# Hybrid layer on one core: modulation loads on GpSimd's queue, shared buffers left to the weights, padded tables cleared at the start

## The chip, the cores and the metric

One core of a Trainium2 chip runs the kernel. The metric is the device time of one execution in microseconds (us), and the median of several runs is compared.

The core has a TensorE (PE: matmuls), a VectorE (DVE), a ScalarE (ACT) and a GpSimd (POOL), and a SyncE (SP) that in this kernel issues DMA transfers only. Each engine works through its own instructions in a fixed order and waits at an instruction until what it needs is there. A transfer is issued by an instruction of one engine, and is then carried out by 16 DMA engines.

## The reference

```python
mod = (jax.nn.silu(c) @ w_ada + b_ada)[:, None, :]      # c: 2048, w_ada: 2048 x 12288
sh1, sc1, g1, sh2, sc2, g2 = jnp.split(mod, N_MOD, axis=-1)

h = rms_norm(x, norm1_g) * (1.0 + sc1) + sh1            # x: 256 x 2048
proj = h @ w_in                                          # 2048 x 4096
q, k, v, u = jnp.split(proj, [ATTN_WIDTH, 2 * ATTN_WIDTH, 3 * ATTN_WIDTH], axis=-1)
...
attn = dilated_attention(q, k, v)                        # 8 heads, three dilations
y = jax.nn.gelu(s5_mixer(u, ...))                        # 64 groups of 16 channels, 64 complex states
ssm = y * jax.nn.sigmoid(y @ w_glu + b_glu)

mixed = jnp.concatenate([rms_norm(attn, attn_out_g), rms_norm(ssm, ssm_out_g)], axis=-1) @ w_out
x = x + g1 * mixed
h2 = rms_norm(x, norm2_g) * (1.0 + sc2) + sh2
ff = jnp.square(jax.nn.relu(h2 @ w_ff1)) @ w_ff2         # 2048 -> 8192 -> 2048
return x + g2 * ff
```

One sequence of 256 positions, all in float32. Nearly 300 MB of weights are read, 100 MB of them `w_ada`.

## The kernel before

**Weights.** A weight product is made of three matmuls over a high and a low part of both factors (`mm3`, L194 to L196). A weight comes in halves of 512 KB (128x1024) through `k.raw` (L179, issued by SP) into the tag `raw`, which has 5 buffers; ACT rounds it into `wh` (L162), DVE takes the rest into `wl` (L137), each with 3 buffers, and both must be done before PE reads them.

**The modulation.** `w_ada` is read in 96 pieces of 1 MB (128x2048). `pump(n)` calls for n pieces, at a rate by stage (`PUMPS`). Pieces of 12 of the 24 blocks go to PE as four matmuls each (L260, into `tr`), the other half to DVE as multiplications with a sum (L159). After four pieces a block of 512 modulation values is done (L271 turns a row into columns, L137 adds the bias into `mod`).

**Places of the pieces.** `ada_raw` gives a piece its place. The first 16 take the places that `FIRST` names: tiles of later stages which stand empty at the start (`Q`, `K`, `U`, `V`, `TO` and `CA` in two halves, `WB0`, `WB1`, `PD`). A later one takes the next name of its stage's list in `RINGS`; where that is `raw`, the piece comes as two halves through `k.raw` and shares the 5 buffers with the weights, and in the stages of the MLP that is the only name. Loads of whole pieces are issued at L242 (`FIRST`) and L248 (`RINGS`), by SP.

```python
FIRST = ("Q", "K", "U", "V", "TO", "TO", "CA", "CA", "WB0", "WB1", "PD", "Q", "K", "TO", "TO", "CA")
RINGS = (("cbc", "K"), ("cbc", "PD", "raw", "raw"), ("cbc", "raw", "raw"), ("HA", "U", "WB0"), ("HA", "PD"))
```

**The start.** Eight pieces give scale and shift of the first 512 columns; beside them ACT squares x (L308) and PE sums (L311, L314). From these come `HA` (L332, L333), and with it the first `w_in` matmul. DVE makes the tables of the S5 mixer out of `bb` and `cc` (tiles `V`, `CA`, `WB2`, `WB3`, `T0`); ACT copies them into padded tables (`padB` in `PD`, `padCs` in `WB0` and `WB1`, cleared by GpSimd at L604), PE multiplies these (L532) and ACT takes the result to the Toeplitz table `TO`, whose empty part GpSimd clears at L612. Two smaller clearings by GpSimd are at L498 (`wpad` in `PD`) and L550 (state `H`).

**What sets the order.** The kernel is written with a tile framework: tiles of one tag share buffers, and a tile's first writer waits for the last reader of the tile before it. A scheduler places the instructions of every engine in a fixed order by a simulated time, so an edit can move instructions of engines that it doesn't name. SP keeps that order for all its loads: a load that waits for its place holds up those behind it. Each queue also has eight counters for loads under way, and its ninth load waits for the first to land.

Of the kernel before, what the change touches and what calls it, by code (L numbers as in the profile page):

```python
# [16 lines left out]
P = 128  # L17
# [9 lines left out]
RAW = 5  # L27
FIRST = ("Q", "K", "U", "V", "TO", "TO", "CA", "CA", "WB0", "WB1", "PD", "Q", "K", "TO", "TO", "CA")
RINGS = (("cbc", "K"), ("cbc", "PD", "raw", "raw"), ("cbc", "raw", "raw"), ("HA", "U", "WB0"), ("HA", "PD"))
PUMPS = (4.0, 2.0, 1.0, 1.0, 0.75, 0.5, 1.0, 0.5, 0.5, 2.5, 1.0, 2.0, 1.0, 0.4)  # L30
# [11 lines left out]
SUB = [0, 2, 1, 3]  # L42
# [75 lines left out]
class _K:  # L118
# [5 lines left out]
    def t(self, tag, shape, dt=F32, bufs=1):  # L124
        self.n += 1
        return self.sb.tile(list(shape), dt, name=f"{tag}_{self.n}", tag=tag, bufs=bufs)
# [72 lines left out]
def _body(nc, tc, I, out, sb, ps):  # L199
    k = _K(nc, tc, I, out, (sb, ps))  # L200
    t, tr = k.t, k.tr
# [16 lines left out]
    sigc = t("sigc", [P, 16])  # L218
    nc.scalar.activation(sigc, col["c"], AF.Sigmoid)
    cpad = t("cpad", [P, 16, 32])  # L220
    nc.vector.memset(cpad, 0.0)
# [8 lines left out]
    def ada_raw(src):  # L230
        if ring["first"] < len(FIRST):
            tag = FIRST[ring["first"]]
            if tag in ("TO", "CA"):
                if tag in halves:
                    raw = halves.pop(tag)[:, 4:8]
# [5 lines left out]
            ring["first"] += 1  # L241
            nc.sync.dma_start(raw, src.rearrange("p (a n) -> p a n", a=4))  # L242
            return [raw]
        ring["i"] += 1
        tag = ring["tags"][ring["i"] % len(ring["tags"])]
        if tag not in ("raw", "T0"):
            raw = t(tag, [P, 4, NB])
            nc.sync.dma_start(raw, src.rearrange("p (a n) -> p a n", a=4))  # L248
            return [raw]
# [134 lines left out]
    s5 = {}  # L384
# [110 lines left out]
    def wb_block(i):  # L495
        if i == 0:
            s5["wpad"] = t("PD", [P, 8, 2, 4, 2, 16])
            nc.gpsimd.memset(s5["wpad"], 0.0)  # L498
        wpad, w, rr = s5["wpad"], i // 2, slice(8 * (i % 2), 8 * (i % 2) + 8)
# [48 lines left out]
    def state_in():  # L548
        H = t("XT", [P, 2, 32, 64])
        nc.gpsimd.memset(H[:, :, :, 0:1].rearrange("p i r c -> p i (r c)"), 0.0)  # L550
        for r2 in range(0, 32, 4):
# [48 lines left out]
    ring["tags"] = RINGS[0]  # L600
    padB = t("PD", [P, 32, 2, 2, 16])
    padCs = [t(f"WB{i}", [P, 8, 2, 2, 4, 16]) for i in range(2)]
    for w in (padB, *padCs):
        nc.gpsimd.memset(w, 0.0)  # L604
    for w in range(2):
# [4 lines left out]
    for b in range(1, 4):  # L610
        tz = toep[32 * b : 32 * b + 32].rearrange("p r g s j -> p (r g) (s j)")
        nc.gpsimd.memset(tz[:, :, 0 : 16 * SUB[b]], 0.0)  # L612
    ca = t("CA", [P, 32, 2, 4, 16])
# [42 lines left out]
    H = state_in()  # L656
# [396 lines left out]
```

## Time and profile before

| | us |
|---|---|
| three runs | 1320.88, 1320.88, 1313.66 |
| median of them | 1320.88 |
| profiled execution, its own time | 1312.4 |
| span of its trace | 1310.6 |
| PE busy in the span | 1210.9 |
| DVE busy | 867.9 |
| ACT busy | 579.7 |
| GpSimd busy | 13.1 |

Busy time counts an engine's own instructions; register, semaphore and DMA-issuing ones are left out. The profiled execution is one more run, 1.3 us below the fastest of the three and 8.5 below their median.

### The profile page before, as it was taken

The page shows a single profiled execution, that of the slowest core. Times are in us where ns is not written, and L with a number is a line of the kernel's source. Part 1 is how long each engine was busy: PE and PEld are TensorE (multiplying, and loading weights), DVE is VectorE, ACT ScalarE, POOL GpSimd, SP SyncE. Part 2 cuts the span into 40 slices and gives each one's busy share as a digit, 9 for nine tenths or more (in the row PEclk, how much of TensorE's full clock was granted, in tenths as well). Part 3 has the DMA queues.
Part 4 walks back from the last instruction along what each step waited for, and adds up shares of the span by engine and source line. Part 5 has one row for each costly group of instructions (what it writes and reads, how often), then busy time and mean ns, then how long its engine had stood idle before and what let it go on. Part 6 is the DMA issues. An engine that isn't in the chain of part 4 may idle for free.

```text
span 1310.6 us, 19312 instructions
## 1 busy us (share of the span) xinstructions
PE 1210.9 (92%) x7618; PEld 1020.9 (78%) x7618; DVE 867.9 (66%) x1383; ACT 579.7 (44%) x783; POOL 13.1 (1%) x12
## 2 busy tenths in 40 slices
PE   5867999999986799798989999999999999999898
PEld 1445766776675799798888888888888888888787
DVE  4666245599778675666768755975576666668754
ACT  3467734333357444344335444443344443343432
POOL 0110000000000000000000000000000000000000
PEclk9988999999879799899999999999999999999999
DMA  9936487747777245657887566765677656677763
GB/s 380 417 141 253 167 329 259 277 162 264 291 286 263 107 153 179 204 193 254 278 289 239 177 192 212 267 202 188 193 239 229 222 185 188 222 218 261 257 208 100
DMA packets 76122, 299.67 MB, mean 229 GB/s; under 512 B 8448, under 2 KB 10752, under 8 KB 68864
## 3 DMA queue, kind: packets, MB, share of 16 engines
q1 hardware_dynamic: 76032, 298.44, 67.0%
q8 instruction: 59, 0.97, 0.3%
q14 instruction: 31, 0.25, 0.1%
HBM read 296.31 MB, written 2.10 MB: 228 GB/s over the span
## 4 chain that ended last, share of the span: by engine, by line
PE 69%; DMA 11%; DVE 6%; ACT 5%; issue 4%; DVEq 0%; ACTq 0%; SPq 0%
PE acc L868 27%; PE acc L870 14%; DMA raw<-w_ada 8%; PE acc L195 4%; PE acc L194 4%; PE acc L196 3%; PE tr L260 3%; PE acc L878 2%; PE acc L877 2%; PE acc L880 2%; DVE wl L137 2%; DMA PD<-w_ada 2%; DVE raw L159 1%; ACT wh L162 1%; PE tr L556 1%
## 5 line engine op out<-in xcount | busy, mean ns | idle before, releaser
L162 ACT ACTIVATE wh<-raw 128x1024 fp32r<-128x1024 f32 x360 | 381.1, 1060 | 540.9 <-PE acc L868 267.8
L137 DVE TENSOR_TENSOR wl<-raw,wh 128x1024 fp32r<-128x1024 f32 x360 | 439.2, 1223 | 265.7 <-ACT wh L162 263.3
L159 DVE SCALAR_TENSOR_TENSOR raw<-raw,cbc 128x1024 f32<-128x1024 f32 x64 | 78.2, 1224 | 63.2 <-DMA raw<-w_ada 62.7
L868 PE MATMUL acc<-CA,wh 128*128 128x512 f32 x384 | 104.6, 396 | 1.7 <-DVE rows L137 0.9
L868 PEld LDWEIGHTS acc<-CA,wh 128*128 128x128 f32 x384 | 65.9, 188 | 11.0 <-issue 1.1
L868 PE MATMUL acc<-TO,wh 128*128 128x512 f32 x256 | 70.3, 396 | 0.0
L868 PE MATMUL acc<-WB,wh 128*128 128x512 f32 x256 | 69.5, 393 | 0.0
L870 PEld LDWEIGHTS acc<-CA,wl 128*128 128x128 f32 x384 | 58.2, 188 | 8.3
L870 PE MATMUL acc<-CA,wl 128*128 128x256 f32 x384 | 60.4, 281 | 0.0
L194 PE MATMUL acc<-wh,HA 128*128 128x512 f32 x128 | 49.4, 413 | 7.0 <-ACT wh L162 6.9
L195 PE MATMUL acc<-wl,HA 128*128 128x512 f32 x128 | 52.9, 414 | 1.4 <-DVE wl L137 1.3
L195 PE MATMUL acc<-wl,HB 128*128 128x512 f32 x128 | 51.7, 404 | 1.7 <-DVE wl L137 1.6
L196 PE MATMUL acc<-wh,HA 128*128 128x512 f32 x128 | 51.3, 405 | 0.0
L196 PE MATMUL acc<-wh,HB 128*128 128x512 f32 x128 | 50.1, 392 | 0.0
L194 PE MATMUL acc<-wh,HB 128*128 128x512 f32 x128 | 46.9, 398 | 1.7 <-ACT wh L162 1.7
L877 PE MATMUL acc<-CA,wh 128*128 128x256 f32 x192 | 48.3, 284 | 0.2 <-ACT CA L162 0.2
L868 PEld LDWEIGHTS acc<-TO,wh 128*128 128x128 f32 x256 | 43.8, 188 | 5.8
L868 PEld LDWEIGHTS acc<-WB,wh 128*128 128x128 f32 x256 | 43.8, 188 | 5.7
L878 PE MATMUL acc<-CA,wh 128*128 128x256 f32 x192 | 47.8, 282 | 0.0
L870 PEld LDWEIGHTS acc<-TO,wl 128*128 128x128 f32 x256 | 39.1, 188 | 5.8
L870 PEld LDWEIGHTS acc<-WB,wl 128*128 128x128 f32 x256 | 38.9, 188 | 5.3
L870 PE MATMUL acc<-TO,wl 128*128 128x256 f32 x256 | 40.6, 280 | 0.0
(332 smaller groups left out, 2467.6 us busy)
## 6 DMA issues: line engine op xcount, KB each, us to landing
raw<-w_ff SPq DMA_DIRECT2D x256, 512.0 KB, 4.2
raw<-w_ada SPq DMA_DIRECT2D x82, 512.0 KB, 5.1
raw<-w_in SPq DMA_DIRECT2D x64, 512.0 KB, 5.5
raw<-w_out SPq DMA_DIRECT2D x32, 512.0 KB, 4.1
PD<-w_ada SPq DMA_DIRECT2D x10, 1024.0 KB, 5.9
HA<-w_ada SPq DMA_DIRECT2D x10, 1024.0 KB, 5.4
cbc<-w_ada SPq DMA_DIRECT2D x8, 1024.0 KB, 7.7
K<-w_ada SPq DMA_DIRECT2D x6, 1024.0 KB, 7.6
```

The costliest lines, as they stand in the source:

```text
L137: return (eng or self.nc.vector).tensor_tensor(out, a, b, op=op)
L159: self.nc.vector.scalar_tensor_tensor(out, a, s, b, op0=op0, op1=op1, accum_out=accum)
L162: self.last_act = self.nc.scalar.activation(out, a, AF.Copy, scale=scale).ins
L194: mm(ps, xh, wh, start=start, stop=False)
L195: mm(ps, xh, wl, start=False, stop=False)
L196: mm(ps, xl, wh, start=False, stop=stop)
L260: k.last_ada = mm(acc[32 * q : 32 * q + 32, :], cpad[:, 4 * g + q, :], raw[:, i, :], start=g == 0, stop=g == 3,).ins
L868: mm(pp[e], hi[:, e, kk], xs[kk].rearrange("p s n -> p (s n)"), start=first and kk == 0, stop=False)
L870: mm(pp[e][:, 0:SEQ], lo[:, e, kk], xs[kk][:, 0], start=False, stop=last and kk == 3)
L877: mm(o, hi[:, e, kk], xs[kk][:, 0], start=first and e + kk == 0, stop=False)
L878: mm(o, hi[:, e, kk], xs[kk][:, 1], start=False, stop=False)
L880: mm(o, lo[:, e, kk], xs[kk][:, 0], start=False, stop=last and e + kk == 4)
```

## The change

The loads of whole pieces (both the `FIRST` ones and those of `RINGS`) are issued by GpSimd in place of SP. Pieces 9 to 16 take other places, `raw` is taken out of the two lists of the `w_in` stages (in the third stage one place is left), and weights alone use `raw` there. The three padded tables `PD`, `WB0` and `WB1` are cleared at the start of the program, and the other three clearings go from GpSimd to DVE. Four lines move, so line numbers in the changed kernel are four higher between the new lines and the old place of the clearing, L260 being L264, for one.

```diff
--- before.py
+++ after.py
@@ -25,8 +25,8 @@
 RQ = 4
 NB = 512
 RAW = 5
-FIRST = ("Q", "K", "U", "V", "TO", "TO", "CA", "CA", "WB0", "WB1", "PD", "Q", "K", "TO", "TO", "CA")
-RINGS = (("cbc", "K"), ("cbc", "PD", "raw", "raw"), ("cbc", "raw", "raw"), ("HA", "U", "WB0"), ("HA", "PD"))
+FIRST = ("Q", "K", "U", "V", "TO", "TO", "CA", "CA", "Q", "K", "V", "TO", "TO", "CA", "CA", "Q")
+RINGS = (("cbc", "K"), ("cbc", "PD"), ("cbc",), ("HA", "U", "WB0"), ("HA", "PD"))
 PUMPS = (4.0, 2.0, 1.0, 1.0, 0.75, 0.5, 1.0, 0.5, 0.5, 2.5, 1.0, 2.0, 1.0, 0.4)
 
 COLS = {}
@@ -217,6 +217,10 @@
 
     sigc = t("sigc", [P, 16])
     nc.scalar.activation(sigc, col["c"], AF.Sigmoid)
+    padB = t("PD", [P, 32, 2, 2, 16])
+    padCs = [t(f"WB{i}", [P, 8, 2, 2, 4, 16]) for i in range(2)]
+    for w in (padB, *padCs):
+        nc.gpsimd.memset(w, 0.0)
     cpad = t("cpad", [P, 16, 32])
     nc.vector.memset(cpad, 0.0)
     mul(cpad[:, :, 0:1].rearrange("p a b -> p (a b)"), sigc, col["c"])
@@ -239,13 +243,13 @@
             else:
                 raw = t(tag, [P, 4, NB])
             ring["first"] += 1
-            nc.sync.dma_start(raw, src.rearrange("p (a n) -> p a n", a=4))
+            nc.gpsimd.dma_start(raw, src.rearrange("p (a n) -> p a n", a=4))
             return [raw]
         ring["i"] += 1
         tag = ring["tags"][ring["i"] % len(ring["tags"])]
         if tag not in ("raw", "T0"):
             raw = t(tag, [P, 4, NB])
-            nc.sync.dma_start(raw, src.rearrange("p (a n) -> p a n", a=4))
+            nc.gpsimd.dma_start(raw, src.rearrange("p (a n) -> p a n", a=4))
             return [raw]
         return [k.raw(src[:, 2 * NB * i : 2 * NB * i + 2 * NB].rearrange("p (a n) -> p a n", a=2), tag) for i in range(2)]
 
@@ -495,7 +499,7 @@
     def wb_block(i):
         if i == 0:
             s5["wpad"] = t("PD", [P, 8, 2, 4, 2, 16])
-            nc.gpsimd.memset(s5["wpad"], 0.0)
+            nc.vector.memset(s5["wpad"], 0.0)
         wpad, w, rr = s5["wpad"], i // 2, slice(8 * (i % 2), 8 * (i % 2) + 8)
         for b in range(4):
             pad_write(lambda gp: wpad[:, :, :, b, gp, :], by_r(bpow[w][:, 3 - SUB[b], :, rr]))
@@ -547,7 +551,7 @@
 
     def state_in():
         H = t("XT", [P, 2, 32, 64])
-        nc.gpsimd.memset(H[:, :, :, 0:1].rearrange("p i r c -> p i (r c)"), 0.0)
+        nc.vector.memset(H[:, :, :, 0:1].rearrange("p i r c -> p i (r c)"), 0.0)
         for r2 in range(0, 32, 4):
             pt = tr()
             pv = pt.rearrange("p (r i c) -> p r i c", r=4, i=2)
@@ -598,10 +602,6 @@
     run(w_in_block(0, [0]), 0)
     run(w_in_block(1, [0]), 0)
     ring["tags"] = RINGS[0]
-    padB = t("PD", [P, 32, 2, 2, 16])
-    padCs = [t(f"WB{i}", [P, 8, 2, 2, 4, 16]) for i in range(2)]
-    for w in (padB, *padCs):
-        nc.gpsimd.memset(w, 0.0)
     for w in range(2):
         nc.sync.dma_start(bpow[w][:, 3], I["bb"][:, w])
     nc.sync.dma_start(c0, I["cc"])
@@ -609,7 +609,7 @@
     toep = t("TO", [P, 32, 2, 4, 16])
     for b in range(1, 4):
         tz = toep[32 * b : 32 * b + 32].rearrange("p r g s j -> p (r g) (s j)")
-        nc.gpsimd.memset(tz[:, :, 0 : 16 * SUB[b]], 0.0)
+        nc.vector.memset(tz[:, :, 0 : 16 * SUB[b]], 0.0)
     ca = t("CA", [P, 32, 2, 4, 16])
     with tc.issue_after(h_end):
         for w in range(2):
```

At the start SP issues the small inputs and x, then before the change the pieces and the weights in one row:

```order
L210 DMA XT_63<-xT 128x1024 x4
L242 DMA Q_81<-w_ada 128x2048
L242 DMA K_87<-w_ada 128x2048
L242 DMA U_93<-w_ada 128x2048
L242 DMA V_165<-w_ada 128x2048
L242 DMA TO_180<-w_ada 128x2048 x2
L242 DMA CA_191<-w_ada 128x2048 x2
L179 DMA raw_307<-w_in 128x1024
L179 DMA raw_313<-w_in 128x1024
L242 DMA WB_58_344<-w_ada 128x2048
```

There the first half of `w_in` (raw) stands behind eight pieces. With the change GpSimd's own row, from its first clearing on, is

```order
L223 MEMSET PD_76 128x2048
L223 MEMSET WB_10_77 128x2048
L223 MEMSET WB_11_78 128x2048
L246 DMA Q_87<-w_ada 128x2048
L246 DMA K_93<-w_ada 128x2048
L246 DMA U_99<-w_ada 128x2048
L246 DMA V_171<-w_ada 128x2048
L246 DMA TO_186<-w_ada 128x2048 x2
L246 DMA CA_197<-w_ada 128x2048 x2
L252 DMA cbc_654<-w_ada 128x2048
L246 DMA Q_350<-w_ada 128x2048
```

and SP's, at the same place:

```order
L210 DMA XT_63<-xT 128x1024 x4
L179 DMA raw_313<-w_in 128x1024
L179 DMA raw_319<-w_in 128x1024
L179 DMA raw_387<-w_in 128x1024
L179 DMA raw_393<-w_in 128x1024
L606 DMA WB_3_68<-bb 128x512
L606 DMA WB_4_69<-bb 128x512
L607 DMA T_6_71<-cc 128x1024
L619 DMA ident_70<-consts 128x160
L179 DMA raw_611<-w_in 128x1024
```

The pieces now stand behind three clearings on an engine of their own, and `w_in`, `bb` and `cc` right behind x.

On DVE, between the first S5 tables (`V`) and the first `CA`, stand before the change the low parts of weights (`wl`), the second block of the modulation (`mod`, `g1c`) and its use on x (`XT`):

```order
L137 TENSOR_TENSOR wl_615<-raw_612,wh_614 128x1024
L137 TENSOR_TENSOR mod_79<-tr_370,small_61 128x4
L157 SCALAR_TENSOR_TENSOR g1c_162<-mod_79,small_61 128x4
L157 SCALAR_TENSOR_TENSOR XT_63<-XT_63,g1c_162,rbc_154 128x256 x4
L137 TENSOR_TENSOR wl_621<-raw_618,wh_620 128x1024
L137 TENSOR_TENSOR wl_669<-raw_666,wh_668 128x1024
L137 TENSOR_TENSOR CA_465<-V_460 128x32x16 x2
```

With the change the same stretch of DVE reads:

```order
L137 TENSOR_TENSOR wl_674<-raw_671,wh_673 128x1024
L137 TENSOR_TENSOR mod_85<-tr_376,small_61 128x4
L157 SCALAR_TENSOR_TENSOR g1c_168<-mod_85,small_61 128x4
L157 SCALAR_TENSOR_TENSOR XT_63<-XT_63,g1c_168,rbc_160 128x256
L612 MEMSET TO_460 32x64x32
L612 MEMSET TO_460 32x64x16
L612 MEMSET TO_460 32x64x48
L157 SCALAR_TENSOR_TENSOR XT_63<-XT_63,g1c_168,rbc_160 128x256 x3
L137 TENSOR_TENSOR wl_743<-raw_740,wh_742 128x1024
L137 TENSOR_TENSOR CA_464<-V_459 128x32x16 x2
```

The three clearings of `TO` now stand ahead of the first `CA`, and one `wl` less.

Much later, where the attention output is normalised (`rs`, `rbc`) while the last pieces of this stage are multiplied (PD and HA at L159), DVE has before the change

```order
L159 SCALAR_TENSOR_TENSOR PD_4025,adap_3884<-PD_4025,cbc_2447 128x2048
L153 TENSOR_SCALAR rs_2466<-tr_3185 128x2
L167 RECIPROCAL rs_2466<-rs_2466 128x2
L159 SCALAR_TENSOR_TENSOR HA_4164,adap_3884<-HA_4164,cbc_2447 128x2048
L137 TENSOR_TENSOR rs_2466<-rs_2466 128x2
L137 TENSOR_TENSOR mod_79<-adap_3884,small_61 128x4
L137 TENSOR_TENSOR rs_2466<-rs_2466 128x2
L157 SCALAR_TENSOR_TENSOR g2c_4460<-mod_79,small_61 128x4
L153 TENSOR_SCALAR rs_2466<-rs_2466 128x2
L137 TENSOR_TENSOR rs_2466<-rs_2466 128x2
L837 COPY rbc_3209<-tr_3210 128x256
```

and with it

```order
L153 TENSOR_SCALAR rs_2447<-tr_3166 128x2
L167 RECIPROCAL rs_2447<-rs_2447 128x2
L137 TENSOR_TENSOR rs_2447<-rs_2447 128x2 x2
L153 TENSOR_SCALAR rs_2447<-rs_2447 128x2
L137 TENSOR_TENSOR rs_2447<-rs_2447 128x2
L159 SCALAR_TENSOR_TENSOR PD_4006,adap_3865<-PD_4006,cbc_2428 128x2048
L837 COPY rbc_3190<-tr_3191 128x256
```

so the whole chain of `rs` now stands ahead of the last two pieces, one of which lies between it and `rbc`.

## Rows read from the trace of the kernel before

**Rows 1.** The page, shares of the chain that ended last, by engine.

```profile
PE 69%; DMA 11%; DVE 6%; ACT 5%; issue 4%; DVEq 0%; ACTq 0%; SPq 0%
```

**Rows 2.** Stretches: length, busy us of each engine, PE clock, DMA share, GB/s.

```profile
0.00:30.00 30.00, 13.89 (x65) 3.44 (x65) 13.52 (x113) 8.29 (x21) 0.20 (x4) 1.00 0.94 375
30.00:60.00 30.00, 26.82 (x142) 15.05 (x142) 19.87 (x34) 15.08 (x24) 5.45 (x3) 0.94 1.02 420
60.00:90.00 30.00, 19.37 (x153) 13.05 (x153) 18.98 (x27) 15.11 (x22) 5.41 (x3) 0.83 0.61 229
90.00:120.00 30.00, 23.36 (x158) 15.13 (x158) 20.90 (x36) 26.92 (x54) 1.81 (x1) 0.89 0.49 184
120.00:350.00 230.00, 225.12 (x1248) 159.17 (x1247) 147.33 (x210) 99.82 (x138) 0.22 (x1) 0.98 0.69 247
```

**Rows 3.** SP's issues at the start: when, how long, what.

```profile
8.99 1.60 SPq L242 DMA_DIRECT2D CA<-w_ada  x2
12.90 2.75 SPq L179 DMA_DIRECT2D raw<-w_in  x2
```

**Rows 4.** PE from its first piece to its first weight matmul: start, busy.

```profile
13.02 1.93 PE L260 MATMUL tr<-Q,cpad 128*32 128x512 f32 x8 [13.02 <-DVE s5t L137]
15.35 1.94 PE L260 MATMUL tr<-K,cpad 128*32 128x512 f32 x8 [0.40 <-DMA K<-w_ada]
...
31.32 3.57 PE L260 MATMUL tr<-TO,cpad 128*32 128x512 f32 x16
34.64 2.01 PE L260 MATMUL tr<-CA,cpad 128*32 128x512 f32 x16
...
39.59 0.50 PE L194 MATMUL acc<-wh,HA 128*128 128x512 f32 x1 [0.17 <-ACT HA L332]
39.93 0.39 PE L195 MATMUL acc<-wl,HA 128*128 128x512 f32 x1
40.16 0.39 PE L194 MATMUL acc<-wh,HA 128*128 128x512 f32 x1
```

**Rows 5.** PE, its two long waits; in brackets the idle time.

```profile
85.50 3.64 PE L532 MATMUL tr<-WB,PD 128*32 128x128 f32 x64 [9.86 <-issue]
...
114.19 1.22 PE L194 MATMUL acc<-wh,HA 128*128 128x512 f32 x2 [5.88 <-ACT wh L162]
```

**Rows 6.** DVE, the S5 chain between 61 and 83 us.

```profile
61.81 0.16 DVE L137 TENSOR_TENSOR mod<-tr,small 128x4 f32<-128x4 f32 x1 [5.45 <-PE tr L271]
...
68.73 1.29 DVE L137 TENSOR_TENSOR CA<-V 128x512 f32<-128x512 f32 x2 [1.33 <-PE tr L260]
...
82.37 1.29 DVE L137 TENSOR_TENSOR CA<-V 128x512 f32<-128x512 f32 x2
```

**Rows 7.** ACT, the copy that L532 waits for.

```profile
83.70 3.44 ACT L162 ACTIVATE WB<-CA 64x768 f32<-64x768 f32 x4 [6.91 <-DVE CA L137]
```

**Rows 8.** GpSimd's clearings, two of the five lines.

```profile
39.51 1.82 POOL L604 MEMSET WB<- 128x2048 f32 x1 [39.07 <-PE tr L260]
...
64.62 5.48 POOL L612 MEMSET TO<- 32x2048 f32 x3 [15.09 <-PE tr L260]
```

**Rows 9.** DVE's clearing, the longest before the change.

```profile
L221 DVE MEMSET cpad<- 128x512 f32 x1 | 0.5, 485 | 0.1
```

**Rows 10.** PE's waits from 120 to 345 us: total, times, longest.

```profile
PE tr L260 <- DMA PD<-w_ada: 0.2, 1, 0.2
```

**Rows 11.** SP's waits over the whole run, in the same form.

```profile
SPq L248 <- PE tr L260: 53.8, 18, 17.0
```

**Rows 12.** DMA issues: KB of one, median us to landing.

```profile
PD<-w_ada SPq DMA_DIRECT2D x10, 1024.0 KB, 5.9
...
cbc<-w_ada SPq DMA_DIRECT2D x8, 1024.0 KB, 7.7
```

**Rows 13.** DVE at the end of the attention stage.

```profile
422.62 2.29 DVE L159 SCALAR_TENSOR_TENSOR PD<-PD,cbc 128x2048 f32<-128x2048 f32 x1 [1.90 <-DMA PD<-w_ada]
...
430.98 2.29 DVE L159 SCALAR_TENSOR_TENSOR PD<-PD,cbc 128x2048 f32<-128x2048 f32 x1 [3.51 <-DMA PD<-w_ada]
```

## The prediction, written before the changed kernel ran

> **What bounds the kernel now.** I read the page first, then the table of stretches, then the start and the two long waits of PE instruction by instruction, and last the waits of SP and DVE. The chain that ended last is PE for 69% of the span and DMA for 11% [rows 1], so a time moves only where PE stands idle, or where work is added to PE or to what it waits for. The stretches show where that is [rows 2]. In the first 30 us PE is busy for 13.89 us, from 60 to 90 for 19.37, from 90 to 120 for 23.36; from 120 to 350 us it is packed, 225.12 of 230.00. The DMA engines are the limit of the first 60 us: their share is 0.94 and then 1.02, at 375 and 420 GB/s, and only then falls to 0.61 and 0.49 [rows 2]. The two long waits after that are not waits for loads. The first, 9.86 us ahead of L532 [rows 5], ends with a copy of ACT at 83.70 [rows 7], which waits for the last CA of DVE's S5 chain at 82.37 [rows 6]. The second, 5.88 us at 114.19 [rows 5], is for a rounded weight of ACT, which is 26.92 of 30.00 us busy there [rows 2]. The changed loads and clearings bear on the start, on this chain, and then on the places of the pieces.
>
> **The start.** The first pieces land 2.33 us apart (Q at 13.02, K at 15.35 with PE waiting 0.40 for its DMA [rows 4]), so 1.05 MB takes 2.33 us. The eighth piece would then be there at 13.02 + 7 x 2.33 = 29.3 us. PE takes the two CA pieces from 34.64 on, the second about 1 us later [rows 4], so the eighth piece has lain ready for some 6 us, behind the sums over x and the TO pieces.
>
> With the change the pieces start after three clearings of 1.82 us on GpSimd [rows 8], 5.5 us, but the DMA engines don't stand still in that time, since x and the weights come from SP. What counts is how many of SP's bytes go ahead of the eighth piece. Before, the weights came behind all eight (the first at 12.90, behind CA at 8.99 [rows 3]). Now the five `raw` buffers and the three `wh` that empty them hold eight halves of `w_in` before the first weight matmul, 4.2 MB, and `bb` and `cc` are 1.0 MB. If all of that goes ahead, it is 5.2 MB, or 5.2 / 1.05 x 2.33 = 11.5 us, and the eighth piece lands at 40.8, 5.2 us after PE took it before. If only the four halves go ahead that SP issues before GpSimd is free, it is 2.1 MB, 4.7 us, and the piece lands at 34.0, inside what it lay ready before: nothing. I take the first end, since the engines are full [rows 2] and no row shows one queue preferred to another: 5 us, between 0 and 5 by these bytes.
>
> No transfer is issued by GpSimd before, so what an issue costs there is not in the trace. Its bounds: no dearer than one from SP (0; two issues of CA took 1.60 us on SP [rows 3]), or one clearing of GpSimd, 1.82 us [rows 8], which I take as the upper end for each. At the start it is hidden behind full DMA engines.
>
> **From the start to the second wait.** DVE's chain waits twice for pieces: 5.45 us ahead of `mod` at 61.81 and 1.33 us ahead of CA at 68.73, which needs the place of the sixteenth piece [rows 6]. The bytes that must come before those are nearly the same as before, on full engines; one piece (`cbc`) moves ahead of them, 2.33 us, so by bytes alone this chain would be about 2 us later, and by PE's order, with the first weight matmul 5 us later, up to 5. The clearings of TO come on top. DVE clears 128x512 in 485 ns [rows 9], 0.95 ns an element; the three have 1024, 2048 and 3072 elements in a partition, so 5.8 us (GpSimd took 5.48 [rows 8]). They stand between `mod` and CA. They need the TO pieces read, which PE does two CA pieces (2.01 us [rows 4]) ahead of the point where CA can be written; 2.0 and the 1.33 of idle time hide 3.3 us of them, and 2.5 are left. A DVE that idles more than before would hide the rest (0), and none hidden is 5.8. Together 5 + 2.5 is 7.5 us for L532. ACT's row of copies behind it is closed up to 114 us, so the second wait ends later by as much: **+7.5 us** at 120 us, between 0 and 11.
>
> The clearing of PD for `wpad` on DVE is 2048 x 0.95 ns = 1.9 us, beside an ACT that sets the pace there: nothing. Clearing the padded tables early takes three steps of 1.82 us [rows 8] off GpSimd's later row; they were done at 39.51 and in the 10 us behind it, long before the copy at 83.70 that writes there [rows 7]: nothing gained.
>
> **The packed stretch, 120 to 350 us.** All that can be won is 230.00 - 225.12 = 4.9 us [rows 2], and of PE's waits there the one for a piece is 0.2 us [rows 10]. SP did stand for 53.8 us in 18 waits for the places of pieces, with weights queued behind it [rows 11], yet the five buffers covered that. I take 1 us won. A piece's new place must be refilled in time: where only `cbc` is left, 46 to 50 weight matmuls stand between two pieces, one every 0.23 us [rows 4], 10.6 us or more. A load into `cbc` took 7.7 us [rows 12] and the piece's matmuls 1.0, so 1.9 us are over, and the dearest issue of 1.82 just fits: 0, or 1 us for each of the five pieces of that stage if it doesn't. The halves that no longer go through `raw` leave the same matmuls: nothing.
>
> **The attention stage.** Here DVE multiplies pieces in PD and HA and waits for them, 1.90 and 3.51 us [rows 13], since a place is refilled only after its use, and each dearer issue is seen. The new order puts the chain of `rs` ahead of a wait of 3.51 and a product of 2.29 us [rows 13]. Up to 5.8 won, up to four issues of 1.82 lost: I take 1 us won, between -6 and +7. In the MLP the loads stay with SP: 0.
>
> **The sum.** 7.5 - 1 - 1 = 5.5, say 6 us on the profiled execution's 1312.4: 1318. The runs lie at 1313.66 and twice at 1320.88, so the four have a mean of 1317, and the median is 8.5 above the profiled one. I count from 1317: **1323 us**, 0.2% above the median shown. Of this kernel a measurement can tell about 1% (13 us) from no change.
>
> **Rivals.** *Faster, with the weights no longer behind the pieces.* With two rows of loads, `w_in`, `bb` and `cc` are there earlier, the S5 chain starts earlier, and PE's 9.86 and 5.88 us [rows 5] and the 4.9 us of the packed stretch shrink. If two thirds of these 20.6 us go, with the start covered as in the lower end, it is -14: 1303. For it speaks the clock: 0.83 and 0.89 in the two stretches with the waits [rows 2], which less waiting would raise. Against it, the S5 chain waits for the sixteenth piece [rows 6], and those loads come through full engines. It decides when the sixteenth piece lands 5 us earlier than now. The Trainium skill, DMA: Bandwidth & Descriptors, section "Issuing engines are not separate DMA queues", says that transfers started by different engines run on the same 16 DMA engines, and that several issuers save the issue time alone; by it this rival has nothing to win at the start, and the share of 1.02 agrees. Chance 0.16.
>
> *Slower, by the issue on GpSimd.* Where a place is refilled just in time, every microsecond of a later issue is a microsecond of PE or DVE. The start's 7.5, five `cbc` pieces at 1 us or more, and some five waits of DVE at 1.82 give 7.5 + 5 + 9 = 21: 1338. It decides from 1.9 us an issue in the packed stretch and from 0 in the attention stage. Against it, the places there have slack by the rows above; for it, GpSimd's row is also in order, so that one late place holds up the next load. The Trainium skill, SBUF — State Buffer, section "SBUF: two separate sides", names a way to it: descriptors of a transfer issued by GpSimd can't be written while DVE runs in a mode that uses the port pair they share, so that the transfer waits, and it advises another issuer. No row here can show that before GpSimd issues loads; by it the prices would lie at this rival's end. Chance 0.25.
>
> *Nothing but scatter.* The second queue brings the pieces no later, the clearings fall into idle time, and PE stays packed: 0 us, 1317. For it, the eighth piece's 6 us of lying ready. Chance 0.22.
>
> **How the numbers follow.** Forecast 0.37, nothing 0.22, slower rival 0.25, faster rival 0.16. The likeliest is 1323, by its own bounds 1312 to 1334. The range takes in most of both other sides, from the faster rival's 1303 to a little above the slower one's 1338: 1303 to 1340. Faster by over 1%, mostly the faster rival: 0.14; slower by over 1%, the slower one and the forecast's upper end: 0.26; within 1%: 0.60.
>
> **What would show it.** In the changed profile the first weight matmul should start near 45 us (39.59 before), L532 near 93, and the second wait end near 122. Transfers from GpSimd should take 6 to 9 us to land later on, PE's waits for pieces between 120 and 350 us stay under 3 us, and DVE show three clearings of some 6 us in all ahead of the first CA. A first weight matmul at 40 us or before proves the step on shared bytes wrong; many waits of PE or DVE for pieces point to the slower rival; an L532 before 85 us to the faster one.

## The result, and the profile after

The changed kernel takes 1304.81 us in the median of 8 runs (1300.72 to 1311.86), the kernel before 1320.79 us in 8 runs beside them (1313.66 to 1323.57). The ratio is 0.9894, interval 0.9865 to 0.9922: 1.1% faster. A second measurement of the changed kernel gave 1305.77 us and 0.9903 (0.9874 to 0.9932). The forecast was 1323 us and slower; the time lies at the lower end of the stated range, on the other side of the kernel before.

The profiled execution has a span of 1303.7 us against 1310.6. The one before is 8.4 us below the median of its eight runs, so the two traces hold 6.9 us of a gain of 14 to 16; the rest stands in neither. The start became later, as forecast; the gain came behind it. The table gives the start of the row that begins or ends each stage, and how much later (+) the changed kernel is there:

| point in the program | before | after | later |
|---|---|---|---|
| first weight matmul | 39.6 | 47.3 | +7.7 |
| L532 (end of the first long wait) | 85.5 | 97.3 | +11.8 |
| end of the second long wait | 114.2 | 125.9 | +11.7 |
| last L194 on `HA` | 303.3 | 305.6 | +2.3 |
| first L836 (`rs` spread into rows) | 436.7 | 426.3 | -10.4 |
| first L868 (in the MLP) | 715.7 | 706.8 | -8.9 |
| end of the span | 1310.6 | 1303.7 | -6.9 |

The third point is not the end of the `w_in` stages: their matmuls on `HB` go on to 322.9 and 326.2 us, and the stage behind it, called the attention stage here, begins with them. Its end is the first use of `rs`. The section on the change calls that the attention output's; it is the S5 mixer's (the sum of squares is `sq2`, the result goes to `CA`), and some of attention follows later.

So the packed stretch gave 9.4 us, the attention stage 12.7, and all that follows took back 3.5.

The chain that ended last, from the page of the changed kernel, against [rows 1]; the DMA's share rose from 11% to 14%, DVE's from 6% to 10%, and PE's fell:

```profile
PE 66%; DMA 14%; DVE 10%; issue 5%; ACT 4%; SPq 0%; DVEq 0%; ACTq 0%
```

The same stretches as [rows 2], in the changed kernel, with the same columns:

```profile
0.00:30.00 30.00, 9.65 (x48) 1.94 (x48) 17.17 (x89) 7.56 (x13) 11.88 (x19) 1.00 0.94 368
30.00:60.00 30.00, 22.89 (x117) 13.25 (x118) 12.19 (x48) 12.73 (x26) 2.62 (x5) 0.83 1.02 422
60.00:90.00 30.00, 23.23 (x132) 14.05 (x124) 26.16 (x34) 12.43 (x18) 0.53 (x1) 0.95 0.60 226
90.00:120.00 30.00, 21.87 (x212) 14.77 (x212) 20.07 (x33) 23.89 (x46) 1.50 (x3) 0.82 0.25 96
120.00:350.00 230.00, 218.89 (x1240) 160.79 (x1240) 151.27 (x220) 108.26 (x156) 13.80 (x27) 0.98 0.71 256
```

The DMA engines are as full in the first 60 us as before (0.94 and 1.02), and PE does less: 9.65 and 22.89 us against 13.89 and 26.82.

PE in the changed kernel, the start, the two long waits and a piece in the packed stretch (start, busy, in brackets the idle time ahead), against [rows 4] and [rows 5]. The trace has two records for each matmul of a piece, so a whole piece is x8 and a half x4:

```profile
15.49 1.94 PE L264 MATMUL tr<-Q,cpad 128*32 128x512 f32 x8 [15.49 <-DMA Q<-w_ada]
19.20 1.94 PE L264 MATMUL tr<-K,cpad 128*32 128x512 f32 x8 [1.76 <-DMA K<-w_ada]
22.92 1.94 PE L264 MATMUL tr<-U,cpad 128*32 128x512 f32 x8 [1.78 <-DMA U<-w_ada]
...
47.26 0.79 PE L194 MATMUL acc<-wh,HA 128*128 128x512 f32 x1 [4.28 <-ACT HA L336]
...
97.27 3.71 PE L536 MATMUL tr<-WB,PD 128*32 128x128 f32 x64 [13.98 <-issue]
...
125.94 1.22 PE L194 MATMUL acc<-wh,HA 128*128 128x512 f32 x2 [5.86 <-ACT wh L162]
...
208.94 1.06 PE L264 MATMUL tr<-PD,cpad 128*32 128x512 f32 x8
209.94 0.50 PE L196 MATMUL acc<-wh,HB 128*128 128x512 f32 x1
...
426.34 1.22 PE L836 MATMUL tr<-ident,rs 128*128 128x128 f32 x4 [2.26 <-DVE rs L137]
```

Pieces from GpSimd's queue are 3.71 us apart, where SP's were 2.33 [rows 4]. The first long wait grew from 9.86 to 13.98 us, the second stayed (5.88 and 5.86).

DVE in the changed kernel, the three clearings of `TO` and the first CA behind them, against [rows 6] and [rows 8]:

```profile
74.46 1.76 DVE L612 MEMSET TO<- 32x2048 f32 x1 [0.60 <-PE tr L264]
76.48 0.91 DVE L612 MEMSET TO<- 32x1024 f32 x1 [0.25 <-issue]
78.07 2.62 DVE L612 MEMSET TO<- 32x3072 f32 x1 [0.68 <-issue]
...
83.03 1.28 DVE L137 TENSOR_TENSOR CA<-V 128x512 f32<-128x512 f32 x2
```

GpSimd's instructions, with a transfer's issue; then the DMA issues by group (KB of one, median us to landing), against [rows 12]:

```profile
2.48 3.58 POOL L223 MEMSET WB<- 128x2048 f32 x2
6.00 0.66 POOL L246 DMA_DIRECT2D Q<-w_ada  x1
...
15.64 0.53 POOL L252 DMA_DIRECT2D cbc<-w_ada  x1 [5.35 <-DMA Q<-w_ada]
```

```profile
cbc<-w_ada POOLq DMA_DIRECT2D x14, 1024.0 KB, 8.1
PD<-w_ada POOLq DMA_DIRECT2D x12, 1024.0 KB, 7.3
HA<-w_ada POOLq DMA_DIRECT2D x10, 1024.0 KB, 7.0
```

An issue on GpSimd takes 0.53 us. PE's waits from 120 to 345 us in the changed kernel (total, times, longest), against [rows 10]; for pieces there is one of 1.2 us:

```profile
PE acc L194 <- ACT wh L162: 5.9, 1, 5.9
PE acc L195 <- DVE wl L137: 1.3, 1, 1.3
PE tr L264 <- DMA PD<-w_ada: 1.2, 1, 1.2
```

### The profile page after: what moved, and what is told of

Read it like the earlier page. It is cut to its first block, busy times and chain, and to the rows that moved or that the text cites. A ratio compares the mean times of both kernels' runs of the same rounds, so it can differ in the third digit from the quotient of the medians.

```text
span 1303.7 us, 19315 instructions
## 1 busy us (share of the span) xinstructions
PE 1199.4 (92%) x7618; PEld 1017.9 (78%) x7618; DVE 876.9 (67%) x1388; ACT 576.6 (44%) x781; POOL 39.4 (3%) x71
## 4 chain that ended last, share of the span: by engine, by line
PE 66%; DMA 14%; DVE 10%; issue 5%; ACT 4%; SPq 0%; DVEq 0%; ACTq 0%
PE acc L868 27%; PE acc L870 13%; DMA raw<-w_ada 8%; PE acc L194 3%; PE acc L195 3%; PE acc L196 3%; DVE wl L137 3%; PE tr L264 2%; PE acc L878 2%; PE acc L877 2%; PE acc L880 2%; DMA ident<-consts 2%; DVE T L137 2%; DMA raw<-w_ff 2%; DVE raw L159 2%
## 5 line engine op out<-in xcount | busy, mean ns | idle before, releaser
L159 DVE SCALAR_TENSOR_TENSOR raw<-raw,cbc 128x1024 f32<-128x1024 f32 x64 | 78.2, 1223 | 65.9 <-DMA raw<-w_ada 65.5
L868 PE MATMUL acc<-CA,wh 128*128 128x512 f32 x384 | 104.8, 396 | 2.6 <-DVE rows L137 1.5
L868 PEld LDWEIGHTS acc<-CA,wh 128*128 128x128 f32 x384 | 65.8, 188 | 12.1 <-ACT wh L162 2.6
L868 PE MATMUL acc<-TO,wh 128*128 128x512 f32 x256 | 70.3, 396 | 0.0
L868 PE MATMUL acc<-WB,wh 128*128 128x512 f32 x256 | 69.6, 394 | 0.0
L194 PE MATMUL acc<-wh,HA 128*128 128x512 f32 x128 | 51.9, 420 | 10.1 <-ACT wh L162 5.9
L196 PE MATMUL acc<-wh,HA 128*128 128x512 f32 x128 | 51.9, 411 | 0.0
L194 PE MATMUL acc<-wh,HB 128*128 128x512 f32 x128 | 48.2, 395 | 0.3 <-ACT wh L162 0.3
L868 PEld LDWEIGHTS acc<-TO,wh 128*128 128x128 f32 x256 | 43.8, 188 | 5.8
L868 PEld LDWEIGHTS acc<-WB,wh 128*128 128x128 f32 x256 | 43.8, 189 | 5.7
L868 PE MATMUL acc<-V,wh 128*128 128x512 f32 x128 | 36.5, 412 | 5.0 <-ACT wh L162 5.0
```

The source lines that it names most:

```text
L159: self.nc.vector.scalar_tensor_tensor(out, a, s, b, op0=op0, op1=op1, accum_out=accum)
L194: mm(ps, xh, wh, start=start, stop=False)
L196: mm(ps, xl, wh, start=False, stop=stop)
L868: mm(pp[e], hi[:, e, kk], xs[kk].rearrange("p s n -> p (s n)"), start=first and kk == 0, stop=False)
```

## The experiments

Three theories stood against each other. *Order of PE:* the gain is that pieces no longer come in halves, so that PE does fewer groups of piece matmuls. A piece's matmul fills 32 of PE's 128 columns, a band; a group is up to four of them, on different bands, right behind each other in PE's row. *Queue:* the gain is that weights stand behind no piece on SP. *Clearings and other order:* the gain comes from what the scheduler moved along, the chain of `rs` for one.

**Places and queue apart.** The first kernel has the new `FIRST` and `RINGS` alone, the second GpSimd's loads alone, the third both; the fourth is the changed kernel with its loads back on SP.

```diff
 e1, e3: FIRST and RINGS as changed
 e2, e3, at L242 and L248:
-            nc.sync.dma_start(raw, ...)
+            nc.gpsimd.dma_start(raw, ...)
 e4, in the changed kernel, at L246 and L252:
-            nc.gpsimd.dma_start(raw, ...)
+            nc.sync.dma_start(raw, ...)
```

> The kernel before with the new places alone (FIRST and RINGS of after); all loads stay with SP and all clearings stay late on GpSimd. Theory A (the gain is the places: pieces that come whole and not as halves through raw cost PE 4.8 us less between 114 and 304 us, and the new order on DVE shortens the attention stage): ratio 0.985 to 0.990, about 1302 to 1308 us. Theory B (the gain is the second queue, which no longer holds weights behind pieces): 0.997 to 1.003. First weight matmul near 38 to 40 us by either.

> The kernel before with the loads of whole pieces issued by GpSimd and nothing else. Theory A: no gain, ratio 1.000 to 1.006, since the pieces still come as halves through raw and the start shares the DMA engines with the weights. Theory B: 0.988 to 0.993. If the late start of the changed kernel (first weight matmul at 47.26 and not 39.59 us) comes from sharing the DMA engines between two queues, it is at 45 to 47 us here; if it comes from the three clearings ahead of the loads on GpSimd, it is at 40 to 42 us.

> New places and loads by GpSimd, the clearings late and on GpSimd as before; its order puts the three padded clearings behind the first eight loads. Against the changed kernel this is the clearings alone. If the clearings at the start cost their 5.5 us: about 1299 us, ratio 0.984, first weight matmul at 41 us. If sharing is the cause: ratio 0.987 to 0.990, first weight matmul at 46 us. Theory A and B both expect a gain here of at least that of the changed kernel.

> The changed kernel with its loads of whole pieces issued by SP again. Theory A: keeps the gain, and wins the start back too (first weight matmul at 40 us): 0.982 to 0.988. Theory B: loses the gain, 0.998 to 1.003.

Places alone: 1307.95 us, ratio 0.9922 (0.9898 to 0.9946). Queue alone: 1330.59, 1.0101 (1.0070 to 1.0132), slower. Both: 1310.40, 0.9940 (0.9918 to 0.9962). The changed kernel on SP: 1307.27, 0.9927 (0.9898 to 0.9955). Most of the gain is there without GpSimd, and the queue by itself costs 1%, so the queue is not the gain's main cause. It costs at the start, where the first weight matmul of its trace comes 13.9 us later than before (53.5), and in PE's waits from 114 to 328 us; rounded weights are late four times, where the kernel before waits three times, 7.4 us, over the same `w_in` work:

```profile
PE acc L194 <- ACT wh L162: 12.3, 4, 6.5
```

The first weight matmul of the third kernel is at 53.1 us, with the loads back on SP at 40.9. In the third the clearings stand behind the eight loads on GpSimd, so the 5.5 us of clearings ahead of the loads are not what delays the start; the loads of two queues beside each other are. The way goes over DVE. Ahead of `HA` it takes the sum over x from PE (`HB`). Where the first pieces are GpSimd's, DVE's order has `dskip` ahead of that, which needs `ident`, a load of 80 KB that SP issues behind halves of `w_in`. In the kernel before, then in the changed one, then in the third:

```profile
30.64 0.42 DVE L151 TENSOR_SCALAR HB<-tr 128x256 f32<-128x256 f32 x1 [14.53 <-PE tr L314]
```

```profile
37.41 0.43 DVE L137 TENSOR_TENSOR dskip<-ident,small 128x256 f32<-128x256 f32 x1 [11.94 <-DMA ident<-consts]
...
40.53 0.41 DVE L151 TENSOR_SCALAR HB<-tr 128x256 f32<-128x256 f32 x1
```

```profile
46.02 0.43 DVE L137 TENSOR_TENSOR dskip<-ident,small 128x256 f32<-128x256 f32 x1 [14.21 <-DMA ident<-consts]
46.37 0.42 DVE L151 TENSOR_SCALAR HB<-tr 128x256 f32<-128x256 f32 x1
```

PE's matmul for that sum starts at 29.90 us in the kernel before and at 35.50 in the changed one, so DVE takes it 0.7 and 5.0 us later; with the loads back on SP it is 0.7 again (30.11 and 30.84). The late start is thus in part the sharing and in part DVE's row behind one small load.

**Only the lists of the rings.** The kernel before with the new `RINGS`, and with its first sixteen places as they were.

```diff
-RINGS = (("cbc", "K"), ("cbc", "PD", "raw", "raw"), ("cbc", "raw", "raw"), ...)
+RINGS = (("cbc", "K"), ("cbc", "PD"), ("cbc",), ...)
```

> The kernel before with RINGS of after alone (raw taken out of the lists of the two w_in stages), FIRST, queue and clearings as before. Theory A says that the gain of the new places lies in pieces that are not taken apart: from the last L507 to the last w_in matmul 129 to 132 us (141.1 before, 131.4 with all new places), ratio 0.991 to 0.995. The rival (the first sixteen places free the S5 tables and the start): nothing won in that stretch, ratio 0.998 to 1.003, and the 10 us belong to FIRST.

1308.77 us, 0.9929 (0.9902 to 0.9956): this one line has what all places together have. The other new places, and the clearings with what they move, add nothing that can be told apart.

The traces put this gain into the packed stretch. The table has its length, from the end of the second long wait to the last L194 on `HA`, the pieces that PE does in it, and PE's time for one:

| kernel | stretch, us | pieces | us a piece |
|---|---|---|---|
| before | 189.1 | 18.5 | 1.39 |
| old `RINGS`, queue alone (e2) | 199.2 | 19.5 | 1.47 |
| old `RINGS`, order of `rs` (e8, below) | 189.3 | 18.5 | 1.39 |
| new `RINGS` alone (e5) | 180.7 | 19 | 1.21 |
| all new places (e1) | 181.5 | 20 | 1.24 |
| changed, on SP (e4) | 181.2 | 20 | 1.16 |
| changed | 179.7 | 18 | 1.16 |

Every kernel with the new `RINGS` has 178.6 to 181.9 us there, except the next one.

**A piece on two bands.** A piece's four matmuls go to four different bands of 32 columns of PE; a half has only two of them. This kernel is the changed one, but from the seventeenth piece on the same sums go two and two to two bands, so that a whole piece is as two halves that stand apart.

```diff
+                        z = 2 * (g % 2) + q % 2 if two else q
-                            acc[32 * q : 32 * q + 32, :], ..., start=g == 0, stop=g == 3,
+                            acc[32 * z : 32 * z + 32, :], ...,
+                            start=g < 2 and q < 2 if two else g == 0, stop=g > 1 and q > 1 if two else g == 3,
```

> The changed kernel, where each piece of blocks after the first sixteen pieces puts its four matmuls on two bands of 32 columns and not on four (the same sums, added up later by the same matmul with ones). If the four matmuls of a whole piece run side by side, and a half or a split piece costs as much PE time as a whole one, each of these 32 pieces costs 0.9 to 1.0 us more: +15 to +20 us where PE is packed (some 18 pieces between 126 and 306 us) and up to +30 in all, about 1322 to 1335 us. If a matmul's cost is its own, wherever it stands: within 3 us of the changed kernel.

1324.81 us, 1.0047 (1.0030 to 1.0064): 19 to 20 us more than the changed kernel, and 190.4 us in the packed stretch at 1.85 us a piece. PE in this kernel; the next row's start shows that a piece now holds PE for 1.84 us:

```profile
206.39 1.91 PE L266 MATMUL tr<-cbc,cpad 128*32 128x512 f32 x8
208.23 0.51 PE L195 MATMUL acc<-wl,HB 128*128 128x512 f32 x1
```

In the queue-only kernel halves go through `raw` as before. PE there: a half (x4) takes 1.05 us, and the next row starts 0.98 later; in the changed kernel the whole piece at 208.94 took 1.06 and 1.00:

```profile
212.29 1.05 PE L260 MATMUL tr<-raw,cpad 128*32 128x512 f32 x4
213.27 0.50 PE L195 MATMUL acc<-wl,HB 128*128 128x512 f32 x1
...
215.76 1.05 PE L260 MATMUL tr<-raw,cpad 128*32 128x512 f32 x4
216.75 0.72 PE L194 MATMUL acc<-wh,HA 128*128 128x512 f32 x2
```

So a half costs PE as much as a whole piece, as long as the other half doesn't stand right behind it. The Trainium skill, TensorEngine Tiling (Array Packing), section Tiling Modes, says that different tiles of the array can execute matmuls in parallel; the 1.06, 1.05 and 1.91 us agree with it.

**The first eight and the first sixteen on SP.** In the changed kernel, what SP issues is the first eight pieces alone, or all that `FIRST` places.

```diff
 e7:
-            nc.gpsimd.dma_start(raw, ...)
+            (nc.sync if ring["first"] <= 8 else nc.gpsimd).dma_start(raw, ...)
 e9:
+            nc.sync.dma_start(raw, ...)        (FIRST alone; RINGS stays on GpSimd)
```

> The changed kernel with the first eight pieces issued by SP ahead of the weights, as before, and the others by GpSimd. If sharing the DMA engines between the two queues makes the late start, the first weight matmul is at 40 to 42 us (47.26 in the changed kernel), L532 at 88 to 93, and the end 3 to 7 us earlier: 1298 to 1302 us, ratio 0.983 to 0.988. If the start is hidden further on anyway: first matmul early, the same end as the changed kernel within 2 us.

> The changed kernel with the first sixteen pieces issued by SP in one row with the weights, and only the pieces of the later stages by GpSimd. If what the queue costs is the sharing of the DMA engines at the start, and what it gives comes later: first weight matmul at 41 to 44 us, end 3 to 8 us earlier than the changed kernel, ratio 0.983 to 0.988. If the queue neither costs nor gives anything that lasts: within 3 us of the changed kernel and of the one on SP, 0.988 to 0.994.

With eight on SP: 1323.69 us, 1.0039 (1.0014 to 1.0063), slower than the kernel before. With sixteen: 1310.54, 0.9942 (0.9920 to 0.9964). In the first, GpSimd no longer waits behind the first eight pieces and issues `cbc` at 6.0, `Q` at 17.2 and `K` at 20.2 us, while SP's eight are on their way. PE waits for the latter, and the first weight matmul comes at 53.24:

```profile
41.58 1.93 PE L264 MATMUL tr<-CA,cpad 128*32 128x512 f32 x8 [2.94 <-DMA CA<-w_ada]
...
53.24 0.79 PE L194 MATMUL acc<-wh,HA 128*128 128x512 f32 x1 [5.44 <-ACT HA L336]
```

This is the sharing of the DMA engines again: whatever a second queue issues early takes bytes from what is needed first.

**The order of `rs` alone.** The kernel before, in which DVE's products of the pieces of the attention stage's end come behind the copy that follows the chain of `rs`.

```diff
+                    with tc.issue_after(k.hold) if k.hold else contextlib.nullcontext():
+                        stt(rf, rf, 1.0, vec["c"][:, o : o + n], ...)
```

> The kernel before with one thing of the attention stage: the products of the last two pieces (PD and HA) stand on DVE behind the chain of rs and rbc and not within it. If the order on DVE there is what shortens the attention stage in every variant, rbc is some 6 us earlier (L836 at 429 to 432 and not at 436.7), and the end is 2 to 6 us earlier, ratio 0.995 to 0.999. If the clock or other waits shorten the stage, L836 stays at 435 or later.

1316.14 us, 0.9982 (0.9964 to 1.0000): at most 0.4%, some 2 us. PE waits 1.48 us for `rs` ahead of the first L836 (L839 in this kernel) at 433.53, where the changed kernel waits 2.26 at 426.34 and the kernel before 7.0 us. The order alone takes 5.5 us of that wait, and its profile has that row 3.2 us earlier, which the time at the end hardly shows.

**The clearings back on GpSimd.** The changed kernel with `TO`, `wpad` and `H` cleared by GpSimd again.

```diff
-        nc.vector.memset(tz[:, :, 0 : 16 * SUB[b]], 0.0)
+        nc.gpsimd.memset(tz[:, :, 0 : 16 * SUB[b]], 0.0)
```

> The changed kernel with the clearings of TO, wpad and H back on GpSimd; the padded tables are still cleared at the start. If the three clearings of TO ahead of the first CA on DVE hold up L532 (97.27 us), it is at 91 to 94 here, and the end up to 4 us earlier, 1300 to 1304 us. If DVE waits for the pieces there anyway: L532 at 96 to 98 and the end within 2 us of the changed kernel.

1310.54 us, 0.9932 (0.9909 to 0.9955), no faster than the changed kernel. PE's first long wait in it is 5.48 us and ends 7.4 earlier than in the changed kernel:

```profile
89.86 3.71 PE L536 MATMUL tr<-WB,PD 128*32 128x128 f32 x64 [5.48 <-issue]
```

The clearings on DVE, with the order that comes of them, do cost some 7 us there; but those 7 us are lost again in the attention stage (L836 at 428.4, 426.3 in the changed kernel). With all loads on SP they cost less: L532 or L536 is at 90.61 us in e1, with the clearings late on GpSimd, and at 92.98 in e4.

**What the queue is worth behind the start, and how far two runs of one kernel differ.** Repeats of the changed kernel (e10), of that with its loads on SP (e11, as e4), and of e14 (e16). Then GpSimd for the rings alone, on top of the new `RINGS` (e12); GpSimd for the last two lists alone, in the changed kernel (e14) and on top of the new `RINGS` (e15).

```diff
 e12, e15: RINGS as changed; e12:
-            nc.sync.dma_start(raw, ...)
+            nc.gpsimd.dma_start(raw, ...)      (RINGS alone)
 e14, e15, loads of RINGS; those of FIRST on SP:
+            (nc.gpsimd if ring["tags"] in RINGS[3:] else nc.sync).dma_start(raw, ...)
```

> The changed kernel once more, beside the one on SP on the same chip. If the queue gives something on top of the places: 2 to 6 us faster than e11, ratio 0.987 to 0.991. If it doesn't: within 2 us of e11, 0.990 to 0.994.

> The changed kernel with all its loads on SP once more, for the comparison with e10: 0.990 to 0.995 by both theories.

> The new RINGS alone, and the pieces of RINGS issued by GpSimd; the first sixteen pieces stay with SP in their old places, the clearings stay as before. If the queue's own gain of about 4 us belongs to the loads after the start, this keeps the early start (first weight matmul 40 to 42 us, L532 at 88 to 91) and wins the attention stage (last w_in matmul to L836 in 119 to 123 us): 1297 to 1302 us, ratio 0.983 to 0.988, faster than the changed kernel. If the queue's gain belongs to the changed kernel's whole order and not to these loads: 0.990 to 0.996.

> The changed kernel with all loads on SP up to the end of the w_in stages and GpSimd for the pieces of the last two lists of RINGS alone. If the queue's gain lies in the attention stage because SP's row there holds pieces behind halves of w_out, the first weight matmul is at 40 to 42 us, last w_in matmul to L836 takes 119 to 122 us, and the end is at 1297 to 1303 us. If that stage's length goes with the granted clock and not with the queue: 125 to 137 us there, with the clock at 1.2 GHz for 35 us or more between 320 and 440 us, and the ratio 0.990 to 0.995.

> The kernel before with the new RINGS, and GpSimd for the pieces of the last two lists of RINGS alone: places of the first sixteen and clearings as before. If what each part does adds up (RINGS -10 us, GpSimd in the attention stage -3 to -5, no late start, no clearings on DVE), 1297 to 1302 us, ratio 0.983 to 0.987, L532 at 88 to 91 us. If an earlier arrival is lost again to the granted clock, as in e13: 0.988 to 0.993, with 35 us or more at 1.2 GHz between 320 and 440 us.

> The kernel of e14 once more, beside e15: ratio 0.986 to 0.990 if its 0.9882 is its own; 0.990 to 0.994 if it was the scatter of one series.

| kernel | us | ratio |
|---|---|---|
| changed, again (e10) | 1305.77 | 0.9903 (0.9874 to 0.9932) |
| changed, loads on SP, again (e11) | 1310.22 | 0.9940 (0.9920 to 0.9961) |
| rings and their queue (e12) | 1306.31 | 0.9901 (0.9879 to 0.9923) |
| changed, queue late (e14) | 1302.61 | 0.9882 (0.9857 to 0.9907) |
| the same again (e16) | 1303.64 | 0.9899 (0.9877 to 0.9922) |
| rings, queue late (e15) | 1298.77 | 0.9865 (0.9844 to 0.9885) |

Beside loads on SP (0.9927 and 0.9940 in the changed kernel, 0.9929 with the new `RINGS` alone), GpSimd as issuer gives 0.2 to 0.6% more in e10, e12, e14, e15 and e16, three to eight microseconds, and nothing in e9, where it issues the same loads of `RINGS` in the changed kernel (0.9942). The intervals of most pairs touch or overlap; that of e15 lies apart from that of e5, and that of e14 from e11's, though not from e4's. For the last two lists a gain is likely, then, and its size is not settled. The last kernel, the kernel before with two lists changed and GpSimd as issuer of the attention stage's pieces, is the fastest measured; its interval overlaps the changed kernel's.

One stretch shows why such small steps are hard to tell: 320 to 440 us, columns as in [rows 2], of e4, of its repeat e11, of the changed kernel and of e13, one row each:

```profile
320.00:440.00 120.00, 96.80 (x784) 80.27 (x785) 96.64 (x183) 73.10 (x128) 0.00 (x0) 0.84 0.69 253
```

```profile
320.00:440.00 120.00, 98.31 (x728) 79.94 (x721) 88.41 (x159) 65.99 (x111) 0.00 (x0) 0.76 0.70 253
```

```profile
320.00:440.00 120.00, 100.44 (x821) 82.37 (x814) 105.04 (x195) 66.67 (x128) 11.18 (x21) 0.89 0.72 271
```

```profile
320.00:440.00 120.00, 97.66 (x778) 80.37 (x778) 98.44 (x188) 64.21 (x119) 11.17 (x21) 0.82 0.71 264
```

The first two are one program. Up to the last L194 on `HA` they agree within 2 us (299.4 and 298.5 there); then the granted clock is 0.84 in one and 0.76 in the other, L836 comes at 424.0 and 435.0, and the spans are 1305.5 and 1313.1.

## Why the prediction was wrong

**Right: the start, and a little short.** First weight matmul forecast near 45, measured 47.26; L532 near 93, measured 97.27; the second wait's end near 122, measured 125.94. The term was +7.5 with an upper bound of 11, and 11.7 came. Its cause was right in part: with two queues on full engines the pieces are 3.71 us apart instead of 2.33, and with the loads back on SP the start is at 40.9. The Trainium skill, DMA: Bandwidth & Descriptors, section "Issuing engines are not separate DMA queues", which the forecast cited against the faster rival, has transfers of all issuers on the same 16 engines, and the 3.71 us agree with it. The eighth piece came near where the forecast had it: PE's weight load for it waits 0.55 us and goes on at 39.34, against 40.8. But the start hung on DVE, which waited for `ident` until 37.41, and this wait the forecast did not have.

**Right in place, mis-sized: the clearings on DVE.** Their length was 5.3 us, forecast 5.8. Of them 2.5 us were to be left uncovered; by e13 they cost some 7, which is more than their length, so at least 2 us are the order around them. The cover was to be PE's two CA pieces and 1.33 us of idle time, but the clearings start only when PE has read `TO` (0.60 us of waiting ahead of the first), and with other work between, CA follows the first by 8.6 us.

**Failed: the packed stretch, forecast -1, measured -9.4.** The step that fell is the sentence "The halves that no longer go through `raw` leave the same matmuls: nothing." They leave the same matmuls and not the same time: a half takes the time of a whole piece. With it fell the bound "All that can be won is 230.00 - 225.12 = 4.9 us", which takes PE's busy time as given. The order of PE could have told it. Ahead of the attention stage it reads in the kernel before and in the changed kernel (other matmuls stand where the dots are):

```
L260 MATMUL tr_2138<-raw_2221,cpad_76 32x512
...
L260 MATMUL tr_2138<-raw_2221,cpad_76 32x512
...
L260 MATMUL tr_2138<-raw_2223,cpad_76 32x512 x2
...
L260 MATMUL tr_2138<-raw_2305,cpad_76 32x512 x2
...
L260 MATMUL tr_2138<-raw_2307,cpad_76 32x512 x2
```

```
L264 MATMUL tr_2123<-cbc_2206,cpad_82 32x512 x4
...
L264 MATMUL tr_2123<-cbc_2288,cpad_82 32x512 x4
```

There two pieces stand in five places before and in two after. Over the program PE's 48 pieces stand in 55 groups before and in 50 after, so some 5 x 1.05 = 5.2 us are won. The trace agrees: PE's time for these lines, before and then after, over the packed stretch (columns length, PE busy, clock, DMA share, GB/s):

```profile
114.20:304.00 189.80, 25.63 (x148) 0.98 0.67 237
```

```profile
125.90:306.40 180.50, 20.84 (x144) 0.98 0.70 246
```

That is 4.8 us of the 9.4, of which some 0.6 is half a piece that the changed kernel does later (148 records against 144). Another 2.2 are idle time: over the stretch PE stood for 3.5 us before and 1.3 after; behind the second long wait it waited 1.5 us for `wh`, 1.0 for `wl` and 0.5 for `PD` before, and only for a piece (1.2 us) after. The last 2.4 us are busy time that I can't assign. As a bound on waits 4.9 us held, but a term of PE's own work was not looked for. That the new `RINGS` make this gain is shown by e5 and e8 (180.7 and 189.3 us); of its two causes e6 shows the first: the same loads and places, with the groups split, cost 20 us. The second, waits that go when pieces leave `raw` to the weights, is read from the traces alone.

**Failed: the attention stage, forecast -1 between -6 and +7, measured -12.7.** In this stage, of the kernel before and of the changed one, columns as in [rows 2]:

```profile
303.30:436.70 133.40, 107.32 (x812) 85.86 (x810) 109.36 (x183) 65.50 (x110) 0.00 (x0) 0.84 0.73 271
```

```profile
305.60:426.30 120.70, 101.92 (x816) 80.77 (x814) 106.91 (x183) 62.27 (x108) 12.23 (x23) 0.92 0.79 294
```

PE's idle time falls by 7.3 us (26.1 to 18.8) and its busy time by 5.4, at a granted clock of 0.92 in place of 0.84. Of the idle time the wait for `rs` gives 4.7, which the forecast had named with up to 5.8 won; the order alone (e8) brings some 2 us in the end. The clock the forecast left out of its sum. Part of it is scatter: the stage takes 124.6 and 136.5 us in two executions of one program (e4 and e11). How much of the 12.7 is the change and how much the execution stays open; the repeat of the changed kernel has 119.9 us there, so it came again, while the kernel with the new `RINGS` alone has 127.8 and with GpSimd for the last two lists as well 122.2. The queue-only kernel, 1% slower in the end, has 121.9 there, so the length of this stage alone doesn't tell the change's part.

**The rivals.** The faster one gave the right time, 1303, by luck: it wanted the two long waits shorter, and they are 13.98 and 5.86 us. The slower one rested on the price of GpSimd's issue. That is 0.53 us, and `PD` lands in 7.3 us from GpSimd and in 7.3 from SP in e4, `HA` in 7.0 and 6.7 (5.9 and 5.4 in the kernel before, whose places are others): its mechanism isn't there. The port pair that the Trainium skill, SBUF — State Buffer, section "SBUF: two separate sides", warns of shows no price in these landings either; whether DVE ran in such a mode here, no run shows. The queue can cost another way, as in e2 (+1.0%) and e7 (+0.4%), by sharing.

**Open.** What the 2.4 us of busy time in the packed stretch are, and why the queue-only kernel waits 12.3 us for rounded weights, was not taken apart further, nor was what takes back the 7 us of e13 in the attention stage beyond its clock of 0.82.

## What to carry to other kernels

Before "the same matmuls, so nothing": count in PE's order how many groups of side-by-side bands there are, since a half-filled group takes as long as a full one, and whatever splits a transfer may split such a group. A second DMA queue adds no bandwidth while the engines are full (422 GB/s from 30 to 60 us here, 420 with one); give it transfers that are not urgent, and watch what was first in the old queue, the small loads that an engine's row stands behind too (`ident`, here). For steps below a per cent compare repeats of one kernel before looking for a cause in the trace of one execution.

## What was not expected of the hardware

Two matmuls of 32 columns side by side took 1.05 us and four took 1.06; four on two bands took 1.91. One program had a granted clock of 0.84 and of 0.76 over the same 120 us in two executions, 7.6 us of span apart, with a difference below 2 us up to that stage. Clearings on GpSimd ahead of its loads went with an earlier start: at the start of the changed kernel the four loads of x took 5.9 us to land in the median, in e3, where the loads come first, 10.9; `ident` let DVE go on at 37.41 and 46.02, and the first weight matmul was at 47.3 and 53.1.
